# MLP second matrices in a three-layer transformer kernel: two of four row blocks as block products of seven instead of eight

## The chip, the cores and the metric

The kernel runs on one core of a Trainium2 chip. A core has a matrix engine (TensorE, PE in the rows), a vector engine (VectorE, DVE), an activation engine (ScalarE, ACT), GpSimd (POOL) and a sync engine (SP) that issues transfers here. Each works through its own list of instructions in order and waits for others by semaphores. SBUF is the on-chip memory; matmuls write to banks in PSUM. The metric is the device time of one execution in microseconds (us); less is better.

## The reference

The reference runs one block of a first model (`first_block`: convolution, stick-breaking attention and cross-attention, merged by gates, then an MLP) and two layers of a second (`hybrid_layer`: forgetting attention and retention, then an MLP). Sequence length is 256 tokens, width 1024, hidden width 4096, all in float32. The change lies in the MLPs, of which there are three:

```python
        h2 = rms_norm(x, g_mlp[l])
        x = x + jnp.square(jax.nn.relu(h2 @ w_up[l])) @ w_down[l]
...
    hid = jnp.square(jax.nn.relu(jnp.einsum('bsd,df->bsf', x, w_ff1)))
    ff = jnp.einsum('bsf,fd->bsd', hid, w_ff2)
    return layernorm(DEEPNORM_ALPHA * x + ff, ln2_g, ln2_b)
```

The second matrix of an MLP, `w_down` or `w_ff2`, has 4096 rows and 1024 columns. Four row blocks of 1024 rows are meant by the title.

## The kernel before

**Weights.** All weight matrices are packed into one stream of chunks, in the order in which they are used (`build_plan`). An up chunk of the later kind has 1024 rows and 256 columns, a down chunk 512 rows and 512 columns; both are 128 partitions x 2048 values and come in two halves of 128x1024 (512 KB). `Stream.load` (L190) has SP load halves into `RB` = 5 raw buffers. `Stream.piece` (L200) splits a half into two parts that are rounded to the matrix engine's format: ACT writes the high part, `whi` (L213), DVE the rest, `wlo` (L214). They go to one of `NB` = 5 pairs of weight buffers; during an MLP `lend` adds a sixth.

**Matmuls.** `mm3` (L320 to L322) makes each product of three matmuls: high by high, high by low, low by high. A unit (`unit_b`, four steps of 128 rows) is 12 matmuls of 512 columns, with 128 tokens as the fixed side and the weights moving. `stream_a` multiplies an up chunk with the weights as the fixed side and 256 tokens moving: 48 matmuls of 256 columns.

**An MLP** (`mlp`, L789). Four chunks of 512 columns of the first matrix come first, held together while the first 128 tokens and then the second 128 pass (`ws`). Their hidden values are transposed by PE in `tok_side`, a generator that advances one step at each `tick`. Then for each group g of 512 hidden values, 2 to 7: two up chunks (ACT takes relu and square, L800 and L801, then ACT and DVE split the values into `hid`, L312 and L306), then the two down chunks of group g-2, each for both halves of the tokens. The last four down chunks are held together. Four PSUM banks (`pd`) gather all eight groups; `half` adds a finished bank to the residual `x` at the end, in the later MLPs with a factor and a layer norm (`ln_half`, L916).

**Order.** Within an engine instructions stand as the code writes them (`manual_schedule`). Units of matmuls are the beat: each `tick` lets the open generators take a step and lets `pump` write out the split of one weight half, or two if fewer than three chunks are ready ahead. `room` says whether a weight buffer is free by then.

## Time and profile before

| | |
|---|---|
| median of 3 runs (lowest, highest) | 1223.91 us (1223.78, 1224.0) |
| the profiled execution's own time | 1223.95 us |
| its span, first to last instruction | 1222.1 us |
| PE busy | 1208.5 us, 99% |
| DVE busy | 734.8 us, 60% |
| ACT busy | 631.6 us, 52% |
| mean granted clock of PE, as a share of full speed | 0.997 |

A busy time is the sum of an engine's instruction times; on PE neighbouring matmuls overlap, so the interval between two starts, and not the length of a row, is what a matmul takes. The chain that ended last is followed back from the last instruction, at each step to what released it. A wait is named by the engine that waited and the instruction that ended the wait. The first MLP lies between about 419 and 598 us of the span.

### The profile page before, as it was taken

Reading aid. Unit: us, or ns where it says so; the run is one execution under the profiler, and the core shown is the slowest. Engines: PE = TensorE matmul, PEld = TensorE weight load, DVE = VectorE, ACT = ScalarE, POOL = GpSimd, SP = SyncE. Lnnn points to the kernel's source line nnn. Section 1 sums busy time; section 2 is a strip of 40 time slices with the busy share of each in tenths; the row PEclk is TensorE's granted clock in tenths of the full one; section 3 lists DMA queues with packets and bytes.
Section 4 is the critical chain, followed back from the end, with each engine's and each line's share of the span. In section 5 each row is a group of like instructions: output and inputs, shape, how many; then the busy total and the mean of one; then the engine's idle time right before and its main releaser. Section 6 shows DMA issues by size and latency. Waiting matters only on the chain.

```text
span 1222.1 us, 18186 instructions
## 1 busy us (share of the span) xinstructions
PE 1208.5 (99%) x7365; PEld 1059.1 (87%) x7365; DVE 734.8 (60%) x941; ACT 631.6 (52%) x887; POOL 26.2 (2%) x45
## 2 busy tenths in 40 slices
PE   8999999999999999999999999999999999999997
PEld 5999987887888888998898889899889888989985
DVE  6488775656666655355476685535567668553452
ACT  6556555545454565455255556545535555653540
POOL 1000000000000000000000100000000010000000
PEclk9999999999999999999999999999999999999999
DMA  8644446665455565556444366555545436655530
GB/s 327 224 148 144 140 156 211 233 195 162 138 172 189 184 243 208 172 172 214 156 166 139 124 214 226 197 188 173 207 130 187 146 118 216 225 193 203 167 126 35
DMA packets 60468, 218.99 MB, mean 179 GB/s; under 512 B 6848, under 2 KB 6992, under 8 KB 60384
## 3 DMA queue, kind: packets, MB, share of 16 engines
q1 hardware_dynamic: 58320, 211.12, 51.6%
q0 software_dynamic: 1776, 6.38, 1.8%
q8 instruction: 58, 0.95, 0.3%
q10 hardware_dynamic: 288, 0.33, 0.1%
q14 instruction: 26, 0.21, 0.0%
HBM read 216.75 MB, written 1.05 MB: 178 GB/s over the span
## 4 chain that ended last, share of the span: by engine, by line
PE 95%; DVE 1%; ACT 1%; DMA 1%; issue 0%; DVEq 0%; POOLq 0%; SPq 0%; ACTq 0%
PE acc L320 17%; PE acc L322 17%; PE acc L321 17%; PE bank L320 13%; PE bank L322 13%; PE bank L321 13%; PE acc L402 2%; PE acc L333 2%; PE aux L329 1%; DMA raw<-in_wpack_dram 1%; PE aux L1082 0%; DMA gmix<-in_g_mix_dram 0%; DVE wlo L214 0%; PE aux L515 0%; PE aux L322 0%
## 5 line engine op out<-in xcount | busy, mean ns | idle before, releaser
L214 DVE TENSOR_TENSOR wlo<-raw,whi 128x1024 fp32r<-128x1024 f32 x392 | 465.0, 1221 | 116.6 <-ACT whi L213 114.5
L213 ACT CAST whi<-raw 128x1024 fp32r<-128x1024 f32 x392 | 394.6, 1048 | 108.7 <-PE bank L322 58.0
L320 PE MATMUL acc<-xTh,whi 128*128 128x256 f32 x1088 | 310.6, 285 | 0.0
L321 PE MATMUL acc<-xTl,whi 128*128 128x256 f32 x1088 | 307.7, 283 | 0.0
L322 PE MATMUL acc<-xTh,wlo 128*128 128x256 f32 x1088 | 307.5, 283 | 0.0
L320 PEld LDWEIGHTS acc<-xTh,whi 128*128 128x128 f32 x1088 | 207.9, 191 | 2.7 <-issue 1.0
L321 PEld LDWEIGHTS acc<-xTl,whi 128*128 128x128 f32 x1088 | 207.9, 191 | 1.0
L322 PEld LDWEIGHTS acc<-xTh,wlo 128*128 128x128 f32 x1088 | 208.0, 191 | 0.0
L320 PE MATMUL bank<-whi,hid 128*128 128x512 f32 x384 | 151.4, 394 | 0.0
L322 PE MATMUL bank<-whi,hid 128*128 128x512 f32 x384 | 151.3, 394 | 0.0
L321 PE MATMUL bank<-wlo,hid 128*128 128x512 f32 x384 | 151.2, 394 | 0.0
L306 DVE TENSOR_TENSOR hid<-r,hid 128x512 fp32r<-128x512 f32 x36 | 24.9, 692 | 166.2 <-ACT hid L312 166.2
L800 ACT ACTIVATE r<-acc 128x512 f32<-128x512 f32 x36 | 21.5, 598 | 147.1 <-PE acc L322 147.1
L320 PE MATMUL acc<-whi,xTh 128*128 128x512 f32 x224 | 90.6, 404 | 0.7 <-ACT xTh L312 0.7
L321 PE MATMUL acc<-wlo,xTh 128*128 128x512 f32 x224 | 88.2, 394 | 1.1 <-DVE wlo L214 1.1
L322 PE MATMUL acc<-whi,xTl 128*128 128x512 f32 x224 | 88.3, 394 | 0.0
L322 PEld LDWEIGHTS bank<-whi,hid 128*128 128x128 f32 x384 | 72.2, 188 | 16.9
L320 PEld LDWEIGHTS bank<-whi,hid 128*128 128x128 f32 x384 | 72.3, 188 | 15.9
L321 PEld LDWEIGHTS bank<-wlo,hid 128*128 128x128 f32 x384 | 72.2, 188 | 16.0
L320 PE MATMUL bank<-whi,xTh 128*128 128x512 f32 (+2 forms) x192 | 68.7, 358 | 0.0
L321 PE MATMUL bank<-wlo,xTh 128*128 128x512 f32 (+2 forms) x192 | 68.1, 354 | 0.0
L322 PE MATMUL bank<-whi,xTl 128*128 128x512 f32 (+2 forms) x192 | 68.0, 354 | 0.0
(263 smaller groups left out, 1457.6 us busy)
## 6 DMA issues: line engine op xcount, KB each, us to landing
raw<-in_wpack_dram SPq DMA_DIRECT2D x388, 512.0 KB, 4.4
raw<-in_wpack_dram SPq DMA_DIRECT2D x4, 528.0 KB, 4.3
gb<-in_ln_g_dram POOLq DMA_DIRECT2D x4, 512.0 KB, 3.9
bb<-in_ln_b_dram POOLq DMA_DIRECT2D x4, 512.0 KB, 6.1
x<-in_x_dram SPq DMA_DIRECT2D x3, 512.0 KB, 7.0
mem<-in_mem_dram SPq DMA_DIRECT2D x2, 512.0 KB, 6.5
out_dram<-x SPq DMA_DIRECT2D x4, 256.0 KB, 2.2
cst<-in_c_dram POOLq DMA_DIRECT2D x1, 898.0 KB, 7.0
```

Source lines behind the costliest of these rows:

```text
L213: nc.scalar.copy(hi, raw)
L214: nc.vector.tensor_tensor(lo, raw, hi.bitcast(F32), op=ALU.subtract)
L306: nc.vector.tensor_tensor(o, x, y, op=op)
L320: nc.tensor.matmul(o, lhsT=lh, rhs=rh, start=first, stop=False, skip_group_check=True)
L321: nc.tensor.matmul(o, lhsT=lh, rhs=rl, start=False, stop=False, skip_group_check=True)
L322: nc.tensor.matmul(o, lhsT=ll, rhs=rh, start=False, stop=last, skip_group_check=True)
L329: nc.tensor.matmul(o[:, h, :], lhsT=q[a][hs[h]], rhs=k[b][hs[h]], start=i == 0, stop=i == 2, skip_group_check=True)
L333: nc.tensor.matmul(o, lhsT=l, rhs=r, start=first, stop=last, skip_group_check=True)
L402: nc.tensor.transpose(o[:, k * 128:(k + 1) * 128], src[:, k * 128:(k + 1) * 128], ident)
L800: nc.scalar.activation(dst, src, AF.Relu)
```

## The change

In each MLP the row blocks 0 and 2 of the second matrix (1024 rows) are seen as four quarters of 512x512, and the hidden values that meet them as four quarters of 128 tokens by 512. A plain product of two such 2x2 grids takes eight products of quarters; seven suffice if some of them are taken between sums and differences of quarters. `PRODUCTS` lists the seven, in order, with the weight quarter that each uses and the one that is first added to it in place.

- `w7` plans the quarters of a block as four loads and seven chunks; `Stream.add` has DVE add two raw halves (f32) ahead of the split.
- `Stream.load` issues a load when the raw buffer `RB` loads back has had its last use, so a quarter's halves stay until the last product that reads them. `RB` is 8 in place of 5. `NB` is 4 in place of 5, and no buffer is lent.
- `seven_side` makes the seven operands from the hidden values (kept whole in `hf`): DVE takes the differences, ACT and DVE split each into high and low. For block 0 it advances during the up chunks that follow, for block 2 during the down chunks of block 1.
- `seven` runs the products: 12 matmuls each, three PSUM banks; products 1, 6, 7 and 4 accumulate into one bank, 5 and 3 into a second, 2 into a third. After each product `gather` has DVE add or subtract the bank as it then stands to or from a quarter of the residual `x`.
- Row blocks 1 and 3 keep eight products; their operands are split by halves of the tokens, and block 1 too is gathered into `x` on its own, block 3 by `half`.
- The order of an MLP is now: four chunks held together, four up chunks, block 0 in seven, four up chunks, block 1, four up chunks, block 2 in seven, block 3.

```diff
-NB = 5
-RB = 5
+NB = 4
+RB = 8
...
+PRODUCTS = ((1, 0, None), (5, 0, 1), (6, 0, 2), (3, 2, None), (7, 1, 2), (2, 3, None), (4, 3, 0))
...
+    def w7(key, w, l, k0, c0, c1):
+        quarters = [(w, l, 128 * (k0 + 4 * i), 4, (c0, c1)[j], 512) for i, j in ((0, 0), (0, 1), (1, 1), (1, 0))]
+        for name, q, s in PRODUCTS:
+            plan.append(((*key, name), quarters if q == 0 and s is None else None, q, s))
...
-        for g in range(2, 8):
-            for c in (2 * g, 2 * g + 1):
+        for pair in range(1, 4):
+            for c in range(4 * pair, 4 * pair + 4):
                 wa((tag, "up", c), wu, l, 256 * c)
+            if pair % 2:
+                w7((tag, "dn", pair - 1), wd, l, 8 * (pair - 1), 0, 512)
             for n in range(2):
-                wb((tag, "dn", g - 2, n), wd, l, 512 * n, 4 * (g - 2))
-        for n in range(2):
-            for g in (6, 7):
-                wb((tag, "dn", g, n), wd, l, 512 * n, 4 * g)
+                for g in (2, 3) if pair == 2 else (6, 7) if pair == 3 else ():
+                    wb((tag, "dn", g, n), wd, l, 512 * n, 4 * g)
...
+        self.loads, self.plan = build_loads()
+        self.last = [0] * len(self.loads)
+        for c, (_, _, _, q, s) in enumerate(self.plan):
+            self.last[q] = c
+            if s is not None:
+                self.last[s] = c
+        self.dma_i = self.split_i = self.added = self.used = self.freed = self.off = 0
...
     def room(self):
         c, h = divmod(self.split_i, 2)
-        return c < len(self.plan) and (h == 1 or self.slot(c) > 0)
+        return c < len(self.plan) and (h == 1 or c < NB + self.freed)
...
     def load(self, upto=RB):
-        while self.dma_i < min(2 * len(self.plan), self.split_i + upto):
-            _, k, n = self.plan[self.dma_i // 2]
+
+        while self.dma_i < 2 * len(self.loads):
+            i, h = divmod(self.dma_i, 2)
+            j, g = divmod(self.dma_i - upto, 2)
+            if j >= 0 and 2 * self.last[j] + g >= self.split_i:
+                return
+            _, _, _, k, _, n = self.loads[i]
...
+    def add(self):
+
+        if self.added == self.split_i and self.added < 2 * len(self.plan):
+            c, h = divmod(self.added, 2)
+            _, _, _, q, s = self.plan[c]
+            if s is not None:
+                a, b = self.raws[2 * q + h], self.raws[2 * s + h]
+                self.nc.vector.tensor_tensor(a, a, b, op=ALU.add)
+            self.added += 1
+
...
         hi, lo = (t[:, h * m:(h + 1) * m] for t in self.tiles[c])
-        raw = self.raws.pop(self.split_i)
+        self.add()
+        raw = self.raws[2 * q + h]
         nc.scalar.copy(hi, raw)
+        self.split_i += 1
+        self.add()
         nc.vector.tensor_tensor(lo, raw, hi.bitcast(F32), op=ALU.subtract)
-        self.split_i += 1
         self.load()
...
-                split(hid[g][0][:, :, ts], hid[g][1][:, :, ts], p.rearrange("p (k t) -> p k t", k=4))
+                nc.scalar.copy(hf[0][:, 4 * g:4 * g + 4, ts], p.rearrange("p (k t) -> p k t", k=4))
+            if t:
+                sides.append(seven_side(0))
+
+        def seven_side(pair):
+
...
+            d, e = (r[:, 512 * i:512 * i + 512].rearrange("p (k t) -> p k t", k=4) for i in range(2))
+
+            def put(name, src):
+                o = new_op(7)
+                split(o[0], o[1], src)
+                ops[pair, name] = o
+
+            put(1, q[0, 0])
+            tt(d, q[1, 1], q[1, 0], ALU.subtract)
+            yield
+            put(5, d)
+            stt(e, d, -1.0, q[0, 0], ALU.mult, ALU.subtract)
+            yield
+            put(6, e)
+            stt(d, e, -1.0, q[0, 1], ALU.mult, ALU.subtract)
+            yield
+            put(3, d)
+            tt(e, q[0, 0], q[1, 0], ALU.subtract)
+            yield
+            put(7, e)
+            yield
+            put(2, q[0, 1])
+            yield
+            put(4, q[1, 1])
+
...
+        def gather(i, j, bank, op):
+
+            x = xtok[:, i, 512 * j:512 * j + 512]
+            stt(x, x, alpha if (i, j) not in first else 1.0, bank, ALU.mult, op)
+            first.add((i, j))
+
+        def seven(pair):
+            bk = {}
+            for name, _, _ in PRODUCTS:
+                while (pair, name) not in ops:
+                    tick(0)
+                x = ops[pair, name]
+                c = "A" if name in (1, 6, 7, 4) else "B" if name == 2 else "C"
+                fresh = c not in bk
+                if fresh:
+                    bk[c] = bank()
+                w = W.get((tag, "dn", pair, name))
+                for k in range(4):
+                    mm3(bk[c], x[0][:, k, :], x[1][:, k, :], w[0][:, k, :], w[1][:, k, :], fresh and k == 0, k == 3)
+                    if k == 1:
+                        tick()
+                W.free()
+                for i, j, op in {1: ((0, 0, ALU.add),), 5: ((1, 1, ALU.subtract),), 6: ((0, 1, ALU.subtract),),
+                                 3: ((0, 1, ALU.subtract),), 7: ((1, 1, ALU.subtract),), 2: ((0, 0, ALU.add),),
+                                 4: ((1, 0, ALU.add),)}[name]:
+                    gather(i, j, bk[c], op)
+                tick()
...
+        def down(bank, n, g, t, w):
+            o = ops[g // 2, t, g % 2]
+            for k in range(4):
+                mm3(bank, o[0][:, k, :], o[1][:, k, :], w[0][:, k, :], w[1][:, k, :], g % 2 == 0 and k == 0,
+                    g % 2 == 1 and k == 3)
...
+        for pair in range(1, 4):
+            for c in range(4 * pair, 4 * pair + 4):
+                p = stream_a((tag, "up", c), xT)
+                cc = c % 4
+                if pair == 2:
...
+                    relu2(hf[2][:, 2 * cc:2 * cc + 2, :], p)
+                    if cc == 3:
+                        sides.append(seven_side(2))
+                else:
...
+                    relu2(rv, p)
+                    for t in range(2):
+                        o = ops[pair, t, cc // 2]
+                        ks = slice(2 * (cc % 2), 2 * (cc % 2) + 2)
+                        split(o[0][:, ks, :], o[1][:, ks, :], rv[:, :, 128 * t:128 * t + 128])
                 tick()
-            if pd is None:
-                pd = [[bank(), bank()] for _ in range(2)]
-            for n in range(2):
-                w = W.get((tag, "dn", g - 2, n))
-                for t in range(2):
-                    down(g - 2, n, t, w)
-                    if t == 1:
-                        W.free()
-                    tick()
+            if pair % 2:
+                seven(pair - 1)
+            if pair == 2:
+                for n in range(2):
+                    p = [bank(), bank()]
+                    for g in (2, 3):
+                        w = W.get((tag, "dn", g, n))
+                        for t in range(2):
+                            down(p[t], n, g, t, w)
+                            if t:
+                                W.free()
+                            if g == 3:
+                                gather(t, n, p[t], ALU.add)
+                            tick()
         ws = [(W.get((tag, "dn", g, n)), g, n) for n in range(2) for g in (6, 7)]
         for t in range(2):
+            p = [bank(), bank()]
             for w, g, n in ws:
-                down(g, n, t, w)
+                down(p[n], n, g, t, w)
                 if t == 1:
...
```

PE's list is 72 matmuls shorter, the sum over six blocks of 96 less 84. On DVE two places matter. In the following rows `wlo` is the split of a weight half, `raw<-raw` the sum of two halves, `hid` and `op` splits of hidden values, `r<-` a difference of operands, `x<-x,bank` a gather, and 128x1024, 128x512 and 128x256 the sizes.

The first place is the first MLP. Before, DVE had there, from the first up chunk's hidden values on, splits of hidden values and of weight halves:

```order
L306 TENSOR_TENSOR hid_4083<-r,hid_4082 128x512
L214 TENSOR_TENSOR wlo<-raw,whi 128x1024 x6
L306 TENSOR_TENSOR hid_4301<-r,hid_4300 128x512
L214 TENSOR_TENSOR wlo<-raw,whi 128x1024 x2
L306 TENSOR_TENSOR hid_4301<-r,hid_4300 128x512
L214 TENSOR_TENSOR wlo<-raw,whi 128x1024 x6
```

Now, from the hidden values of the last up chunk ahead of the first seven-product block (two operations of 256) up to the second gather, it has:

```order
L339 TENSOR_TENSOR op_4275<-r,op_4275 128x256
L339 TENSOR_TENSOR op_4276<-r,op_4276 128x256
L339 TENSOR_TENSOR op_4355<-r,op_4355 128x512
L248 TENSOR_TENSOR wlo<-raw,whi 128x1024
L339 TENSOR_TENSOR op_4369<-hf,op_4369 128x512
L232 TENSOR_TENSOR raw<-raw 128x1024
L248 TENSOR_TENSOR wlo<-raw,whi 128x1024
L342 SCALAR_TENSOR_TENSOR x_3502<-x_3502,bank 128x512
L339 TENSOR_TENSOR op_4382<-hf,op_4382 128x512
L232 TENSOR_TENSOR raw<-raw 128x1024
L248 TENSOR_TENSOR wlo<-raw,whi 128x1024 x2
L342 SCALAR_TENSOR_TENSOR x_3502<-x_3502,bank 128x512
```

The first gather, which reads the bank that products 1 and 6 accumulate into, now stands behind four operand splits, two weight splits and a sum; the second behind one operand split, two weight splits and a sum more.

The second place is the seven-product block of the third row block, in the same MLP. Before, the same stretch of DVE's list read:

```order
L214 TENSOR_TENSOR wlo<-raw,whi 128x1024 x2
L306 TENSOR_TENSOR hid_4895<-r,hid_4894 128x512
L214 TENSOR_TENSOR wlo<-raw,whi 128x1024 x6
L306 TENSOR_TENSOR hid_5093<-r,hid_5092 128x512
L214 TENSOR_TENSOR wlo<-raw,whi 128x1024 x2
L306 TENSOR_TENSOR hid_5093<-r,hid_5092 128x512
```

Now, from the last up chunk's hidden values up to the last split ahead of the third gather:

```order
L339 TENSOR_TENSOR op_5135<-r,op_5135 128x256
L339 TENSOR_TENSOR op_5136<-r,op_5136 128x256
L248 TENSOR_TENSOR wlo<-raw,whi 128x1024
L232 TENSOR_TENSOR raw<-raw 128x1024
L248 TENSOR_TENSOR wlo<-raw,whi 128x1024
L342 SCALAR_TENSOR_TENSOR x_3502<-x_3502,bank 128x512
L232 TENSOR_TENSOR raw<-raw 128x1024
L248 TENSOR_TENSOR wlo<-raw,whi 128x1024 x2
L342 SCALAR_TENSOR_TENSOR x_3502<-x_3502,bank 128x512
L248 TENSOR_TENSOR wlo<-raw,whi 128x1024
L232 TENSOR_TENSOR raw<-raw 128x1024
L248 TENSOR_TENSOR wlo<-raw,whi 128x1024
```

Each gather stands behind two splits and a sum, and there are no operand splits between them.

## Rows read from the trace of the kernel before

**Rows 1.** The page: span, and engines with busy us, share and instructions.

```profile
span 1222.1 us, 18186 instructions
...
PE 1208.5 (99%) x7365; PEld 1059.1 (87%) x7365; DVE 734.8 (60%) x941; ACT 631.6 (52%) x887; POOL 26.2 (2%) x45
```

**Rows 2.** The page: chain that ended last, share of the span by engine.

```profile
PE 95%; DVE 1%; ACT 1%; DMA 1%; issue 0%; DVEq 0%; POOLq 0%; SPq 0%; ACTq 0%
```

**Rows 3.** PE's waits: us in total, times, longest; first and last of seven.

```profile
PE acc L402 <- DVE ht L309: 1.3, 1, 1.3
...
PE aux L320 <- ACT Tq L312: 0.3, 1, 0.3
```

**Rows 4.** Stretches of the first MLP: busy us by engine, granted clock, DMA share, GB/s.

```profile
core 0: us, PE busy (x) PEld busy (x) DVE busy (x) ACT busy (x) POOL busy (x), PEclk, DMA share, GB/s
...
465.00:487.00 22.00, 22.00 (x143) 19.95 (x142) 10.42 (x10) 11.40 (x14) 0.00 (x0) 1.00 0.50 177
...
510.00:533.00 23.00, 23.00 (x148) 20.86 (x147) 9.50 (x9) 9.40 (x12) 0.00 (x0) 1.00 0.60 203
```

**Rows 5.** Timeline of PE, 499 to 523 us: start, length, instruction.

```profile
499.75 0.39 PE L320 MATMUL bank<-whi,hid 128*128 128x512 f32 x1
...
510.81 0.28 PE L320 MATMUL acc<-xTh,whi 128*128 128x256 f32 x1
...
522.31 0.39 PE L320 MATMUL bank<-whi,hid 128*128 128x512 f32 x1
```

**Rows 6.** Timeline of DVE, 456 to 606 us; a row of xN spans N instructions.

```profile
457.56 5.76 DVE L214 TENSOR_TENSOR wlo<-raw,whi 128x1024 fp32r<-128x1024 f32 x5 [0.26 <-ACT whi L213]
...
602.02 0.69 DVE L306 TENSOR_TENSOR x<-bank,x 128x512 f32<-128x512 f32 x1
602.63 1.22 DVE L214 TENSOR_TENSOR wlo<-raw,whi 128x1024 fp32r<-128x1024 f32 x1
...
605.01 0.41 DVE L306 TENSOR_TENSOR ta<-bank,cst 128x256 f32<-128x256 f32 x1
605.34 0.42 DVE L306 TENSOR_TENSOR on<-bank,cst 128x256 f32<-128x256 f32 x1
```

**Rows 7.** Groups of DVE by line and shape: busy us, mean ns, idle before.

```profile
L916 DVE SCALAR_TENSOR_TENSOR x<-x,bank 128x512 f32<-128x512 f32 x16 | 11.0, 684 | 30.2 <-PE bank L322 30.2
```

**Rows 8.** Timeline of ACT behind the up chunk that ends at 516.56 us.

```profile
516.75 0.60 ACT L800 ACTIVATE r<-acc 128x512 f32<-128x512 f32 x1 [7.44 <-PE acc L322]
...
518.04 0.62 ACT L312 CAST hid<-r 128x512 fp32r<-128x512 f32 x1
```

**Rows 9.** Timeline of DVE behind the same chunk.

```profile
518.70 0.69 DVE L306 TENSOR_TENSOR hid<-r,hid 128x512 fp32r<-128x512 f32 x1 [7.57 <-ACT hid L312]
```

**Rows 10.** Timeline of ACT, 462 us: a cast that waited for its raw half.

```profile
462.46 1.05 ACT L213 CAST whi<-raw 128x1024 fp32r<-128x1024 f32 x1 [1.13 <-DMA raw<-in_wpack_dram]
```

**Rows 11.** Timeline of DVE, 423 us, first chunks of the first MLP.

```profile
423.67 5.76 DVE L214 TENSOR_TENSOR wlo<-raw,whi 128x1024 fp32r<-128x1024 f32 x5
```

**Rows 12.** Timeline of PE there: first matmul of the fourth chunk.

```profile
427.49 0.48 PE L320 MATMUL bank<-whi,xTh 128*128 128x512 f32 x1
```

**Rows 13.** Stretches at the start, columns as in rows 4.

```profile
8.00:12.00 4.00, 3.40 (x12) 2.04 (x13) 3.29 (x6) 3.68 (x5) 0.00 (x0) 0.74 1.02 416
12.00:16.00 4.00, 3.04 (x11) 2.09 (x9) 3.33 (x4) 3.37 (x5) 2.30 (x4) 0.83 1.03 411
```

**Rows 14.** Timeline of PE at the start.

```profile
8.08 1.32 PE L402 MATMUL acc<-ident,ht 128*128 128x128 f32 x8 [1.30 <-DVE ht L309]
9.91 0.80 PE L320 MATMUL acc<-whi,xTh 128*128 128x512 f32 x1 [0.51 <-ACT xTh L312]
...
12.30 0.63 PE L321 MATMUL acc<-wlo,xTh 128*128 128x512 f32 x1
12.73 0.63 PE L322 MATMUL acc<-whi,xTl 128*128 128x512 f32 x1
```

**Rows 15.** The page: DMA issues, count, KB each, median us to landing.

```profile
x<-in_x_dram SPq DMA_DIRECT2D x3, 512.0 KB, 7.0
```

More of the change, by code (lines that the diff above doesn't have):

```diff
@@ L148, in build_plan, with build_loads @@
     return plan
+def build_loads():
+    loads, chunks = [], []
+    for p in build_plan():
+        if len(p) == 7:
+            chunks.append((p[0], p[4], p[6], len(loads), None))
+            loads.append(p[1:])
+            continue
+        key, quarters, q, s = p
+        if quarters is not None:
+            base = len(loads)
+            loads.extend(quarters)
+        chunks.append((key, 4, 512, base + q, None if s is None else base + s))
+    return loads, chunks
 def pack_weights(inputs):
-    plan = build_plan()
-    flat = np.empty(sum(128 * k * n for _, _, _, _, k, _, n in plan), np.float32)
+    loads = build_loads()[0]
+    flat = np.empty(sum(128 * k * n for _, _, _, k, _, n in loads), np.float32)
     o = 0
-    for _, w, l, r0, k, c0, n in plan:
+    for w, l, r0, k, c0, n in loads:
         for h in range(2):
@@ L786, in block_kernel, with mlp @@
     yst.close()
-    def mlp(tag, xT, half, on_start):
+    def mlp(tag, xT, half, on_start, xtok, alpha):
         st = ExitStack()
@@ L792, in mlp, with new_op @@
         hp = pool(st, "mlp" + str(tag))
-        W.lend(pool(st, "wts" + str(tag)), (tag, "dn", 7, 1))
-        hid = {}
-        def new_hid(g):
-            hid[g] = tuple(hp.tile([128, 4, S], F32R, tag=f"hid{i}", name=f"hid{i}", bufs=3) for i in range(2))
+        ops, hf = {}, {}
+        def new_op(n):
+            t = hp.tile([128, 2, 4, 128], F32R, tag=f"op{n}", name=f"op{n}", bufs=n)
+            return t[:, 0], t[:, 1]
         def relu2(dst, src):
@@ new lines, in mlp @@
+        first = set()
+        def gather(i, j, bank, op):
[23 more added lines that the diff above has]
+                tick()
@@ L915, in ln_half @@
             cell[t] = sm.tile([128, 2], F32, tag="lsum", name="lsum")
[L916 removed]
+        nc.vector.scalar_tensor_tensor(out=xtok[:, t, ns], in0=xtok[:, t, ns], scalar=alpha, in1=bank, op0=ALU.mult,
                                        op1=ALU.add, accum_out=cell[t][:, n:n + 1])
```

62 lines of the change are left out of this document (21 added, 41 removed).

## The prediction

> **What bounds the kernel now.** I read the profile in this order: engines, chain, TensorE's waits, then stretches of the first MLP. TensorE (PE) is busy 1208.5 us of a span of 1222.1, VectorE (DVE) 734.8, ScalarE (ACT) 631.6 [rows 1]. 95% of the chain that ended last is PE [rows 2], and PE's waits for another engine are seven rows, the first of 1.3 us and the last of 0.3, 5.9 us in all [rows 3]. So PE sets the time, and a matmul taken away is worth its issue interval while the others keep up. In the first MLP they do: DVE is busy 10.42 of 22 and 9.50 of 23 us in two stretches with PE full [rows 4]. That slack is an average; the question is where in a stage the added work falls.
>
> **Prices.** In the second matrix 48 matmuls of 512 columns start from 499.75 up to 510.81, 0.230 us each; two up chunks of 48 matmuls take from 510.81 to 522.31, 5.75 us each [rows 5]. On DVE I use the interval between starts, not the duration: five splits of 128x1024 end 5.76 us after the first starts, one lasts 1.22, so (5.76-1.22)/4 = 1.14; 512 wide 602.63-602.02 = 0.61; 256 wide 605.34-605.01 = 0.33 [rows 6].
>
> **Part 1, matmuls removed.** One row block took 8 units of 12 matmuls, 96 x 0.230 = 22.1 us; now 7 x 12, a product of 12 costing 2.76 and the block 19.3. Two blocks in three MLPs: 72 matmuls, 16.6 us. That is the gain if nothing else waits.
>
> **Part 2, DVE work added, per MLP.** Splits of weight halves: 14 per block in place of 8, so 12 more. Sums: four products of each block have one, on two halves, 16 more. No row shows a sum in f32; the nearest is the split, a subtraction of the same shape on two operands, and I take its 1.14 us; from above its full 1.22, from below half of it, 0.57. Gathers: 18 of 0.61 (nearest row: the accumulation into x, 684 ns long [rows 7]). Operands: 14 splits and 8 differences of 512 and 16 splits of 256 replace 16 splits of 512. Together 13.7+18.2+11.0+13.4+5.3-9.8 = 51.8, or 155 us in three MLPs: DVE would be busy some 71% of the span. On average that fits, so the stage decides.
>
> **Part 3, the first seven-product block of an MLP.** Let 0 be the time at which PE ends the last of the four up chunks ahead of it. A chunk that ends at 510.81+5.75 = 516.56 is followed by ACT's relu at 516.75, its square, its cast at 518.04, and DVE's split of the hidden values at 518.70 [rows 8, 9]: 2.1 us; the cast is now half as wide, and I take 1.9. DVE runs in its written order, and from the second chunk's end (-11.5+1.9 = -9.6) it has, with everything it needs at hand:
> - ahead of the third chunk's hidden values: two operations of 256, four of 512, four of 1024, 0.67+2.44+4.56 = 7.7
> - ahead of the fourth's: two of 256, four of 512, three of 1024, 0.67+2.44+3.42 = 6.5
> - then two of 256, two of 512, three of 1024 and the first gather to its end, 0.67+1.22+3.42+0.69 = 6.0.
>
> That is 20.2 us, so the first gather ends at 10.6. PE waits for it: the third product accumulates into the bank that the gather of the first reads. PE has done two products by 5.5, and waits 5.1. From there DVE has one gather behind two or three operations of 1024, about 4 us against PE's 2.76: the next gathers end at 15.2, 19.2, 23.1 and, behind two splits of the next chunk, 26.1. Products three to seven start at 10.7, 15.3, 19.3, 22.1 (into a fresh bank) and 26.2; the last ends at 28.9. **28.9 against 22.1: 6.8 us lost.**
>
> The raw halves add nothing to this: the next chunk's loads take the slots whose last reader comes first (the third quarter's, free at about 9 and 12), and a load needs 3.7 us (a split from 457.56 ends at 458.78; the half that follows in its slot is cast at 462.46 [rows 6, 10]). It is wanted at 23, so there are 7 us of cover.
>
> **Part 4, the second block.** Its operands are made earlier, beside the down chunks of the second row block, so only sums, splits and gathers are in its queue. DVE starts on the last up chunk's values at 1.9, waits for ACT's cast of the next weight half until 3.2, then split, sum, split, gather: 7.3. PE waits 1.8 there, then 1.3, 1.3 and 1.4; the last product ends at 25.1. **3.0 lost.** Beside those down chunks (22 us) DVE has 8 splits, 15 operations of 512 and so 18 us, paced by PE; I cost that at nothing, and at up to 1 us a block if it slips.
>
> **Part 5, the rest.** Four weight buffers for six in the MLPs and five elsewhere, eight raw halves for five. Outside the MLPs DVE's order hardly moves, since the pump looks three chunks ahead. I cost it at nothing; the cover is PE's work on chunks already split, and it is thin where four chunks are held at once: in the first MLP five splits run from 423.67 to 429.4 [rows 11] while PE starts on the fourth chunk at 427.49 [rows 12]. If it goes, 1 to 2 us in each of some five places.
>
> **Sum.** 3 x (6.8+3.0) = 29.4 us lost, on the profiled execution's own 1223.95 (span 1222.1 plus 1.85 around it; the median is 1223.91): **1253**. With the full 1.22, 0.69 and 0.42 us for each operation the two chains grow by 3.3 and 1.1: 1266. With sums at 0.57 they lose 4.0 and 2.3: 1234. I stay with the intervals, since the nearest rows are back to back like these.
>
> The Trainium skill, "VectorE: DVE Perf Modes", section "The DRAIN you can't avoid", says that the next Vector operation does not start until the pipe has emptied, and exempts only operations that are not held; by it the full duration is the price and the sum 1266. Here starts lie 0.08 us closer than the duration [rows 6], so the trace goes with the exemption.
>
> **Rivals.** *The look-ahead suffices (faster).* DVE idles for over half of two stretches [rows 4]; were it far enough ahead that each gather is free when its product ends, the 16.6 us come whole: 1207. It decides at one point: the 20.2 us of DVE between the second up chunk and the first gather must fit into 9.6+5.5 = 15.1, and the second block's 7.3 into 5.5. Against it: four weight buffers hold a product's splits back until PE has used up a chunk, and sums stand ahead of gathers in a strict order. 0.07. If gain and waits cancel, no change: 0.05.
> *The second block costs nothing, or sums are cheap.* Then the second gives 2.8 and the first costs 6.8: 1223.95+3x4.0 = 1236; with cheap sums 1234. 0.14.
> *The clock falls.* Between 8 and 16 us the granted clock was 0.74 and 0.83 [rows 13], behind PE waits of 1.3 and 0.5 us, and matmuls of 512 columns came 0.43 us apart (12.30 to 12.73) in place of 0.23 [rows 14]: 1.2 GHz for 2.4. A product would take 5.2 us. One or two at that rate are hidden, since DVE sets the pace (the third would end at 15.9, the fourth start then in place of 15.3). All five products behind the first wait at that rate would end the blocks at 36.7 and 33.3, 48 us more in all, 1301; I take a third of that, 1269. 0.13.
> The Trainium skill, "TensorE: Matmul & The Clock Gate", section "HAM oscillation", says that idle gaps on TensorE put its clock back to half; by it the long wait at the third product could do so, which is this rival. The trace of before has no such gap after the start.
> *Weights arrive late.* One block's quarters hold all eight raw halves, and loads of the same size took 7.0 us from issue to landing [rows 15]; 3 us behind each block is 18: 1271. 0.03.
> *The change doesn't do what it says.* PE's order is 72 matmuls shorter, so it does.
>
> **How the numbers follow.** Forecast 1253 with 0.58 (1244 to 1266); smaller loss 0.14 (1230 to 1244); clock 0.13; late weights 0.03; no change 0.05; faster 0.07. A measurement of this kernel tells some 0.2% from none, 2.4 us. Slower 0.58+0.14+0.13+0.03 = 0.88, same 0.05, faster 0.07. The range leaves out the faster and unchanged cases and the outer part of the clock's: 1236 to 1273.
>
> **What would show it.** Right: in the changed profile DVE is the first among PE's waits, some 10 us at each first block and 6 at each second; the longest wait, about 5 us, stands ahead of a first block's third product and ends with the gather; DVE has no idle time from some 10 us ahead of the block to its fifth gather; outside the MLPs nothing moves. Wrong: waits on DMA or ACT there, a granted clock below 1 in those stretches, sums at half the split's price, or PE without waits and the time near 1207.

## The result and the profile after

| | before | after |
|---|---|---|
| median (lowest, highest) | 1223.85 us (1223.62, 1224.0) | 1255.62 us (1255.44, 1255.72) |
| ratio, 95% interval | | 1.026 (1.0242 to 1.0277) |
| profiled execution: own time, span | 1223.95, 1222.1 us | 1255.72, 1253.9 us |
| PE, DVE, ACT busy | 1208.5, 734.8, 631.6 us | 1204.3, 887.8, 687.0 us |
| mean granted clock | 0.997 | 0.989 |

The change makes the kernel 31.8 us slower. The page of the kernel after gives each engine's busy time with its share and instructions, and further down the chain that ended last, by engine. They answer to [rows 1, 2].

```profile
PE 1204.3 (96%) x7293; PEld 1049.2 (84%) x7293; DVE 887.8 (71%) x1145; ACT 687.0 (55%) x977; POOL 26.2 (2%) x45
...
PE 82%; DVE 11%; ACT 3%; issue 3%; DMA 1%; DVEq 0%; POOLq 0%; SPq 0%; ACTq 0%
```

The 72 matmuls are gone (7365 to 7293), and DVE has the 71% that the prediction gave it. But DVE now holds 11% of the chain where it held 1%: PE stands and waits for it somewhere. PE's waits (us in total, times, longest) say for what:

```profile
PE bank L353 <- DVE x L342: 28.4, 14, 5.1
PE bank L353 <- ACT whi L245: 7.7, 7, 1.1
```

Both rows are new against [rows 3]. The first is a matmul that accumulates into a bank which a gather (DVE, line 342, into `x`) still has to read. The second names ACT's casts of the weights, but that is only how the profile puts down a wait for several things: by the starts and ends in the timelines all 21 waits of the two rows end 0.15 us behind the end of a gather. They are all waits for gathers. The timeline of PE in the first block of the first MLP (start, length, instruction; in brackets the idle time ahead and what ended it) shows where:

```profile
471.59 0.40 PE L355 MATMUL bank<-whi,op 128*128 128x512 f32 x1
477.04 0.76 PE L353 MATMUL bank<-whi,op 128*128 128x512 f32 x1 [5.05 <-DVE x L342]
477.60 0.63 PE L354 MATMUL bank<-wlo,op 128*128 128x512 f32 x1
478.03 0.63 PE L355 MATMUL bank<-whi,op 128*128 128x512 f32 x1
...
485.84 0.47 PE L353 MATMUL bank<-whi,op 128*128 128x512 f32 x1 [1.02 <-DVE x L342]
...
492.79 0.47 PE L353 MATMUL bank<-whi,op 128*128 128x512 f32 x1 [1.11 <-DVE x L342]
...
495.65 0.28 PE L353 MATMUL acc<-xTh,whi 128*128 128x256 f32 x1
```

The block's first matmul starts at 466.25, and the third product, first to use a bank again, starts at 477.04 behind a wait of 5.05. DVE's timeline beside it shows the gather for which it waits, and what stands ahead of the next one:

```profile
473.94 1.22 DVE L232 TENSOR_TENSOR raw<-raw 128x1024 f32<-128x1024 f32 x1
475.08 1.22 DVE L248 TENSOR_TENSOR wlo<-raw,whi 128x1024 fp32r<-128x1024 f32 x1
476.21 0.68 DVE L342 SCALAR_TENSOR_TENSOR x<-x,bank 128x512 f32<-128x512 f32 x1
476.81 0.69 DVE L339 TENSOR_TENSOR op<-hf,op 128x512 fp32r<-128x512 f32 x1
477.41 1.22 DVE L232 TENSOR_TENSOR raw<-raw 128x1024 f32<-128x1024 f32 x1
478.55 2.42 DVE L248 TENSOR_TENSOR wlo<-raw,whi 128x1024 fp32r<-128x1024 f32 x2
480.89 0.68 DVE L342 SCALAR_TENSOR_TENSOR x<-x,bank 128x512 f32<-128x512 f32 x1
```

Row follows row without idle time: a sum (`raw<-raw`), splits (`wlo`), an operand, and between them the gathers, 4.68 us from the first to the second. Product one ended 2.8 us behind the block's start; its gather came 7 us later, for no reason but its place in DVE's queue. From PE's first start to its last and one more matmul, the first block takes 29.4 us (783.36 to 812.78 and 1100.58 to 1129.97 in the other MLPs, the same), and the second 25.45. Before, the eight products of row block 0 stood in two pieces. Here are the first start of each and the first start behind it, in the first MLP of the kernel before:

```profile
454.46 0.39 PE L320 MATMUL bank<-whi,hid 128*128 128x512 f32 x1
...
465.61 0.28 PE L320 MATMUL acc<-xTh,whi 128*128 128x256 f32 x1
...
477.05 0.40 PE L320 MATMUL bank<-whi,hid 128*128 128x512 f32 x1
...
488.25 0.28 PE L320 MATMUL acc<-xTh,whi 128*128 128x256 f32 x1
```

That is 11.15+11.20 = 22.35 us, and row block 2 took 22.3 in the same way. The two blocks lose 3 x (7.05+3.15) = 30.6 of the 31.8 us; the other 1.2 lie outside them.

### The profile page after: what moved, and what is told of

Same layout as the page of the kernel before. It is cut to its first block, busy times and chain, and to the rows that moved or that the text cites. A ratio compares the mean times of both kernels' runs of the same rounds, so it can differ in the third digit from the quotient of the medians.

```text
span 1253.9 us, 18383 instructions
## 1 busy us (share of the span) xinstructions
PE 1204.3 (96%) x7293; PEld 1049.2 (84%) x7293; DVE 887.8 (71%) x1145; ACT 687.0 (55%) x977; POOL 26.2 (2%) x45
## 4 chain that ended last, share of the span: by engine, by line
PE 82%; DVE 11%; ACT 3%; issue 3%; DMA 1%; DVEq 0%; POOLq 0%; SPq 0%; ACTq 0%
PE acc L353 16%; PE acc L355 15%; PE acc L354 15%; PE bank L353 10%; PE bank L354 10%; PE bank L355 9%; DVE wlo L248 5%; DVE raw L232 2%; PE acc L435 2%; PE acc L366 2%; DVE x L342 1%; DVE op L339 1%; ACT whi L245 1%; PE aux L362 1%; DMA raw<-in_wpack_dram 1%
## 5 line engine op out<-in xcount | busy, mean ns | idle before, releaser
L248 DVE TENSOR_TENSOR wlo<-raw,whi 128x1024 fp32r<-128x1024 f32 x428 | 512.2, 1220 | 127.0 <-ACT whi L245 125.8
L245 ACT CAST whi<-raw 128x1024 fp32r<-128x1024 f32 x428 | 433.5, 1049 | 160.8 <-DVE raw L232 53.4
L353 PE MATMUL bank<-whi,op 128*128 128x512 f32 x360 | 146.7, 408 | 36.0 <-DVE x L342 28.4
L354 PE MATMUL bank<-wlo,op 128*128 128x512 f32 x360 | 144.4, 401 | 0.0
L355 PE MATMUL bank<-whi,op 128*128 128x512 f32 x360 | 144.2, 401 | 0.0
L353 PEld LDWEIGHTS bank<-whi,op 128*128 128x128 f32 x360 | 69.4, 193 | 59.6 <-ACT whi L245 35.4
L355 PEld LDWEIGHTS bank<-whi,op 128*128 128x128 f32 x360 | 69.3, 192 | 16.5
L354 PEld LDWEIGHTS bank<-wlo,op 128*128 128x128 f32 x360 | 69.5, 193 | 14.9
L232 DVE TENSOR_TENSOR raw<-raw 128x1024 f32<-128x1024 f32 x48 | 58.5, 1220 | 0.5
L339 DVE TENSOR_TENSOR op<-r,op 128x256 fp32r<-128x256 f32 (+1 forms) x72 | 34.1, 508 | 33.6 <-ACT op L345 33.6
```

The costliest lines, as they stand in the source:

```text
L232: self.nc.vector.tensor_tensor(a, a, b, op=ALU.add)
L245: nc.scalar.copy(hi, raw)
L248: nc.vector.tensor_tensor(lo, raw, hi.bitcast(F32), op=ALU.subtract)
L339: nc.vector.tensor_tensor(o, x, y, op=op)
L353: nc.tensor.matmul(o, lhsT=lh, rhs=rh, start=first, stop=False, skip_group_check=True)
L354: nc.tensor.matmul(o, lhsT=lh, rhs=rl, start=False, stop=False, skip_group_check=True)
```

## The experiments

A ratio stands with its 95% interval; all runs are against the kernel before, which took 1223.6 to 1223.9 in each set. This table gathers what the timelines show of the two blocks (row blocks 0 and 2) in the first MLP, measured as above; e1 to e12 are the runs below. Without any wait a block of seven is 84 x 0.232 = 19.5 us.

| run | first block | second block | time, us |
|---|---|---|---|
| before (eight products) | 22.35 | 22.3 | 1223.9 |
| after | 29.4 | 25.45 | 1255.6 |
| e2: only the second block in seven | eight | 25.4 | 1234.2 |
| e3: no sums | 22.4 | 20.6 | 1220.2 |
| e4: a bank for each product | 24.4 | 20.5 | 1227.3 |
| e5: sums on GpSimd | 36.0 | 29.6 | 1288.3 |
| e6: PE kept busy in the long wait | 29.4 | 25.5 | 1255.7 |
| e7: sums by adding DMA | 33.3 | 31.9 | 1290.0 |
| e8: operands earlier | 28.6 | 25.5 | 1253.4 |
| e9: sums doubled | 39.2 | 34.3 | 1307.3 |
| e10: gathers ahead of weights | 27.0 | 22.5 | 1238.4 |
| e11: e10, e8 and splits put off | 23.9 | 22.5 | 1235.2 |
| e12: splits let in by a table | 21.5 | 21.0 | 1236.5 |

**Is it the buffers?** The kernel before with the changed buffer counts and nothing else.

```diff
-NB = 5
-RB = 5
+NB = 4
+RB = 8
```

(and the call that lends a sixth buffer is gone.)

> The kernel before with four weight buffers and eight raw halves, nothing lent; plain products everywhere. DVE's queue in the seven-product blocks is the cause (theory): the buffers cost nothing, 1224 us, within 1222 to 1227. Rival, that fewer weight buffers hold PE up: a good part of the 32 us comes here, 1235 or more.

Measured 1224.84, ratio 1.001 (1.0001 to 1.0019): 1.0 us, between 0.1 and 2.3. The buffers by themselves are not the cause.

**Does each block cost what it was said to?** The first block goes back to eight products; the second stays in seven.

```diff
-            if pair % 2:
+            if pair == 3:
...
```

> The changed kernel with row block 0 back to eight products and only row block 2 in seven. Theory: the first block's operand splits stand in the same DVE queue and make it the dear one; what is left is three second blocks of 25.4 us in place of 22.1, 1224 + 3 x 3.3 and some 1 to 2 us around them, 1235. Rival, that a seven-product block costs the same wherever it stands: half of the 32 us, 1240. Rival, that the second blocks cost nothing by themselves: 1216.

Measured 1234.18, ratio 1.0085 (1.007 to 1.010). The second blocks cost 10.4 us, which leaves 21.4 for the first ones. The waits of the second block are those of the kernel after: the longest is 1.7.

**Is it the sums?** The kernel without them; four of its products use the bare quarter.

```diff
-            if s is not None:
-                a, b = self.raws[2 * q + h], self.raws[2 * s + h]
-                self.nc.vector.tensor_tensor(a, a, b, op=ALU.add)
```

> The changed kernel without the sums of raw halves (four of the seven products use the bare quarter). Theory: with 16 x 1.14 us less per MLP ahead of the gathers, the first block ends at about 21.2 us and the second at about 20.3 in place of 29.4 and 25.4: 1217, within 1212 to 1222. Rival, that PE waits for buffers, banks or the clock and not for DVE's time: 1245 or more.

Measured 1220.23, ratio 0.9971 (0.9959 to 0.9982). Less 54.7 us of DVE (48 x 1.14) makes 35.4 us less time. PE's first wait shrinks to this:

```profile
PE bank L350 <- DVE x L339: 8.3, 9, 1.7
```

So even with sums for nothing the change would have won 3.6 of its 16.6 us: the first block, with its operands, its six more splits and its gathers, takes 22.4, as long as with eight products.

**Is it the shared bank?** Every product gets a bank of its own, so that no matmul waits for a gather. The sums over products are left out by this.

```diff
-                fresh = c not in bk
-                if fresh:
-                    bk[c] = bank()
+                fresh = True
+                bk[c] = bank()
```

> The changed kernel with a fresh PSUM bank for every product, so that no product waits for the gather of an earlier one (the sums over products are left out). DVE's work and order are the same. Theory: PE then waits only for the splits in the same queue; the first block ends at about 25.3 in place of 29.4, the second at 21.5 in place of 25.4, in all 1233 to 1234. Rival, that the splits themselves are what PE waits for: 1255. Rival, that the shared bank is all of the loss: 1208.

Measured 1227.33, ratio 1.003 (1.0019 to 1.0041), better than I expected. DVE's queue is as it was: the gather that started at 476.21 starts here at 476.15, but nobody waits for it. 28.3 of the 31.8 us are paid only where a gather stands between two products in one bank. What is left is another wait, for the weights themselves:

```profile
PE bank L354 <- DVE wlo L248: 12.2, 11, 1.8
```

**Can GpSimd take the sums?**

```diff
-                self.nc.vector.tensor_tensor(a, a, b, op=ALU.add)
+                self.nc.gpsimd.tensor_tensor(a, a, b, op=ALU.add)
```

> The changed kernel with the sums on GpSimd in place of DVE, in the same places. Theory: DVE has 18 us less per MLP; if a sum takes GpSimd up to some 2.5 us and does not slow DVE, the blocks end at about 21.2 and 20.3 us: 1217. If GpSimd is slower or takes DVE's memory port, sums come late and the time lies between 1225 and 1255. Rival, that DVE's time is not the cause: 1250 or more.

Measured 1288.29, ratio 1.0525 (1.0508 to 1.0543), in the rival's range, but not for the rival's reason, and far above what I gave to a slow GpSimd. The groups of instructions by line and shape (busy us, mean ns of one, idle before) show two costs:

```profile
L232 POOL TENSOR_TENSOR raw<-raw 128x1024 f32<-128x1024 f32 x48 | 132.8, 2788 | 360.0 <-DVE wlo L248 360.0
L339 DVE TENSOR_TENSOR op<-r,op 128x256 fp32r<-128x256 f32 x48 | 48.4, 1048 | 30.2 <-ACT op L345 30.2
L342 DVE SCALAR_TENSOR_TENSOR x<-x,bank 128x512 f32<-128x512 f32 x54 | 36.8, 682 | 5.3 <-PE bank L355 5.3
L342 DVE SCALAR_TENSOR_TENSOR r<-r,hf 128x512 f32<-128x512 f32 x12 | 21.3, 1772 | 0.0
```

A sum takes 2.79 us on GpSimd (1.22 on DVE), and the splits behind it wait for it. And DVE's own operations get longer: the split of 256 goes from 420 ns to 1048, the difference `r<-r,hf` from 683 to 1772. The gather, of the same instruction and shape as that difference, stays at 682 (680 in the kernel after). The two differ in where their second operand lies: `hf` in SBUF, `bank` in PSUM. DVE is busy 905.3 us here and 887.8 in the kernel after: taking the sums off DVE gave it more to do, not less.

**Can the DMA take them?** Each sum is an adding DMA between raw halves, issued as soon as the earlier reader of the same quarter has been split.

```diff
...
-                self.nc.vector.tensor_tensor(a, a, b, op=ALU.add)
+                self.nc.gpsimd.dma_start(out=a, in_=b, accum_op=ALU.add)
...
```

> The sums of weight quarters are made by adding DMAs (out = out + in, between raw halves in SBUF, issued from GpSimd's queue) in place of DVE instructions, each issued as soon as the product ahead of it that reads the same quarter has been split; all else is as in the kernel after. Theory (DVE's work in the block, with the sums in it, sets the time): DVE's queue is as in the run without sums, which took 1220, so 1218 to 1230 if the adding DMA lands in about the 4 to 5 us that a raw half takes from DRAM, since products five and six then follow a split by one such landing each. Rival (the sums must be somewhere, and where they move they are waited for): landings of 10 us or more put ScalarE's and DVE's splits of the second and third product late by some 5 us each in each of six blocks, and the time is 1250 or more, with PE waits that name the casts of the weights and no longer the gathers.

Measured 1289.97, ratio 1.0538 (1.052 to 1.0556): the rival's number without its condition, landings of 10 us or more. The page (DMA issues: count, KB each, median us to landing), and the timelines of GpSimd and of DVE in the first block:

```profile
raw<-raw POOLq DMA_DIRECT2D x48, 512.0 KB, 5.4
```

```profile
480.51 0.85 POOL L237 DMA_DIRECT2D raw<-raw  x1 [15.19 <-DVE wlo L252]
```

```profile
487.02 1.23 DVE L252 TENSOR_TENSOR wlo<-raw,whi 128x1024 fp32r<-128x1024 f32 x1 [5.07 <-ACT whi L250]
...
493.50 0.68 DVE L347 SCALAR_TENSOR_TENSOR x<-x,bank 128x512 f32<-128x512 f32 x1
```

A landing takes 5.4 us, nearly what I had allowed. But the block's last sum adds into the quarter that the product named 2 (the sixth) has just split, so it is issued at 480.51 and no sooner, and DVE's queue, which runs in order, stands 5.07 us at the split of that sum with the gathers behind it. PE stands too, 5.61 us, until 494.32, 0.15 us behind the gather that starts at 493.50. (PE's rows name casts for 33.5 us of waits, the rival's sign, but these waits too end 0.15 us behind a gather.) The sums left DVE's busy time and not its queue.

**Does the clock cost anything?** In the long wait of the first block PE's clock falls. Stretches of the first MLP in the kernel after (us, busy of PE, PEld, DVE, ACT, POOL, granted clock, DMA share, GB/s):

```profile
474.00:478.00 4.00, 0.96 (x2) 0.83 (x3) 4.00 (x6) 1.05 (x1) 0.00 (x0) 0.56 0.42 118
478.00:482.00 4.00, 4.00 (x12) 3.13 (x11) 4.00 (x5) 2.94 (x3) 0.00 (x0) 0.58 0.58 188
482.00:486.00 4.00, 2.98 (x14) 2.13 (x13) 3.97 (x5) 1.05 (x1) 0.00 (x0) 1.00 0.81 265
```

In the third product matmuls start 0.43 us apart (477.60 to 478.03 above), the lower level of 1.2 GHz. The next run fills most of the wait with matmuls into a bank that nobody reads.

```diff
+                if name == 6 and pair == 0:
+                    spare = acc()
+                    for i in range(18):
+                        nc.tensor.matmul(spare, lhsT=y[0][:, i % 4, :], rhs=y[0], start=True, stop=True,
+                                         skip_group_check=True)
+                y = x
```

> The changed kernel with 18 matmuls into an unused bank between the second and third product of each first block, so that PE is at work during the wait of 5 us (their result is not used). Theory: the clock stays up, the third product takes 2.8 us in place of 4.8, and the fourth starts when its gather allows, 0.3 us sooner: 1254.7, three times 0.3 below the changed kernel. Rival, that the clock's fall is part of the loss: 3 x 2 us sooner, 1250.

Measured 1255.67, ratio 1.026 (1.0245 to 1.0275). Its PE timeline:

```profile
472.18 4.29 PE L900 MATMUL acc<-op 128*128 128x512 f32 x18
477.40 0.48 PE L353 MATMUL bank<-whi,op 128*128 128x512 f32 x1 [0.93 <-DVE x L342]
...
482.08 0.47 PE L353 MATMUL bank<-whi,op 128*128 128x512 f32 x1 [1.64 <-ACT whi L245]
```

The third product starts where it did (10.79 us into the block in both), runs at full clock (granted 1.00 from 478 to 482 us) and ends 2.0 us sooner, and the fourth then waits 1.64 us and starts only 0.15 us sooner. The row names a cast, but the wait ends 0.15 us behind the second gather, which the fourth product needs. The clock's fall in this block costs nothing.

**How much of DVE's added time is paid?** Each sum is followed by a second instruction of its size.

```diff
                 self.nc.vector.tensor_tensor(a, a, b, op=ALU.add)
+                self.nc.vector.tensor_tensor(a, a, a, op=ALU.max)
```

> Each of the 48 sums is followed by one more DVE instruction of its size that leaves the sum as it is (the larger of it and itself), so DVE has twice the cost of the sums and nothing else changes. Without the sums the time was 1220.2, with them 1255.6: 35.4 us for 48 x 1.14 = 54.7 us of DVE, 0.65 us of the end for each us of the sums. Theory (the sums take idle time of DVE ahead of the blocks first and are then paid whole): the second dose is paid at more than the first, 0.65 to 1.0: 1291 to 1310. Rival (it is less the sums' own time than the one step in which a product's weights wait for its sum, so that work in DVE's queue is mostly hidden): 0.4 or less, 1277 or below.

Measured 1307.31, ratio 1.0677 (1.0659 to 1.0695). No sums 1220.2, sums once 1255.6, twice 1307.3: of the first 54.7 us of DVE 65% are paid, of the second 95%. By the pages (span less busy time, in which instructions that overlap count once, and are not summed) DVE idles 386.1 us without the sums, 366.1 with them and 361.2 with twice their cost: the first dose still finds idle time of DVE, the second hardly any. TensorE's clock falls more often in this run, too (mean granted clock 0.972 for 0.989); how much of the second dose is the clock's is not shown.

**Is it the block's late start on DVE?**

```diff
-            yield
-            yield
+            if t == 0:
+                yield
+                yield
...
-            r = hp.tile([128, D], F32, tag="r", name="r", bufs=2)
+            r = hp.tile([128, 512], F32, tag="rs", name="rs", bufs=1)
...
```

> The operands of the first block of seven begin about 6 us earlier: the second half of hidden block 0 is transposed two steps earlier, and the differences have a 2 KB tile of their own, so the seven operands are made beside the first up chunks of the stage and not its last ones. The work of every engine stays the same. Theory (DVE's queue sets the first block: it is packed from 9.6 us ahead of the block to its end, while between 442 and 456.7 it idles 5 to 6 us): the idle time is filled, the first gather and all behind it come 3 to 6 us earlier, the wait ahead of the third product shrinks from 5.05 us to 2 or less, and the three first blocks end 3 to 5.5 us earlier each: 1239 to 1247. Rival (inside the block a product needs more of DVE than PE's 2.8 us, and the block's end is set by that pace from its own first gather, or by the weights that four buffers let in): the third product's wait goes and comes back at the fourth and fifth, and the time stays at 1253 to 1256.

Measured 1253.36, ratio 1.0239 (1.0224 to 1.0254). By its time that is the rival's, but the trace says that the edit hardly did what it was for: DVE is packed from 450.81 where it was from 456.66, but from 442 us to there it had idled for 6.1 us and still idles for 4.7, so only 1.4 us of work were moved forward, and the first gather starts at 475.94 for 476.21. It leaves open what a truly earlier start would bring.

**Is it the order in DVE's queue?** Inside the block only the next product's weights are split ahead.

```diff
+AHEAD = 2
...
-            if self.room():
+            if self.room() and (ahead is None or self.split_i < 2 * self.used + ahead):
...
-                        tick()
+                        tick(1, AHEAD)
...
```

> Only the order of DVE's (and ScalarE's) queue inside a block of seven changes: there the stream splits no more than one product's weights beyond the running one (two halves, in place of the six that the four buffers let in), so that a gather stands behind one or two splits and sums and no longer behind those of three products; what is put off comes after the block. The work of every engine is the same. Theory (a gather is late because of the weights queued ahead of it, of which some belong to chunks behind the block): laying the measured starts of DVE's rows (1.14 for a sum or split, 0.61 and 0.33 for operands, 0.60 for a gather) end to end in the new order gives 24.9 us for the first block (29.9 by the same count in the old order, 29.4 measured) and 22.9 for the second (25.6, and 25.4 measured), 7.7 less per MLP: about 1232, 1228 to 1238. Rival (lookahead of weights is what keeps PE fed, and with two halves each product waits for its own split): the waits name the casts and splits of the weights, and the time is 1250 or more.

Measured 1238.43, ratio 1.012 (1.0105 to 1.0135). No engine has less to do, and 17.2 of the 31.8 us are gone. The two waits of the kernel after have given way to these:

```profile
PE bank L355 <- DVE wlo L249: 12.0, 14, 1.2
PE bank L354 <- DVE x L343: 8.3, 3, 2.8
```

So more than half of the loss is a matter of order: splits for products and chunks further on stood ahead of gathers that PE needed at once. It fell 6 us short of my count. In the first MLP the wait of 2.78 us ahead of the third product was again followed by the lower clock (rows 0.43 us apart from 475.39 on), which here put off the end; in the two other MLPs the same wait was not.

**What else stands ahead of the gathers?** To e10 and e8 this run adds that the splits of the hidden values of the last two up chunks go behind the block.

```diff
+                    if cc > 1:
+                        lates.append(late)
...
             if pair % 2:
                 seven(pair - 1)
+                while lates:
+                    lates.pop(0)()
```

> As the run with the gathers ahead of the weights, and besides the operands of the first block begin earlier, as in the run of that name, and the splits of hidden block 1's last two up chunks, which nothing needs in the block, go behind it. Theory (all that counts is what stands in DVE's queue ahead of the gathers that PE needs): by the same count of DVE's rows the first block takes 22.3 us, its first gather ends 6.2 us behind the block's start (10.6 measured in the kernel after), and the second block 22.9 as in the other run: three MLPs at 45.2 in place of 54.8, 28.8 us less: about 1227, 1224 to 1234, so at best what the kernel before took. If DVE's total work and not its order holds the blocks, it gives nothing over the other run.

Measured 1235.18, ratio 1.0094 (1.0077 to 1.0111). The first block falls to 23.9, and the remaining wait for a gather is one of 1.1 to 1.2 us in each MLP; 15.1 us of PE's waits are now for splits of weights. But it put off the same splits behind the second block too, where block 3 needs them at once: from the second block's end to block 3's the kernel after takes 22.95 us and this one 24.5, three times 1.6 given back.

**How far does order carry?** Splits are let in one half at a time by a table, and two gathers for which no product waits go behind the block.

```diff
+CAPS = (7, 7, 8, 9, 9, 11, 11, 12, 12, 14, 14, 15, 15, 15)
...
-                    gather(i, j, bk[c], op)
+                    held.append((name not in (3, 2), i, j, bk[c], op))
+                    if held[-1][0]:
+                        gather(*held.pop()[1:])
...
```

> The same seven products, in the run before this one's order with four edits to DVE's queue in the blocks: the splits of the weights are let in one half at a time by a table, so that each gather stands where PE has just ended its product; the gathers of the products named 3 and 2, for which no later product waits, go behind the block; the first operand of hidden block 0 is split one step earlier; and the late splits of hidden block 3 go back to where they were, since the products right behind the second block read them (1.3 us lost there in each MLP). Theory (order of DVE's queue): by the count of rows that gave 23.4 and 22.3 us for the last order (23.9 and 22.5 measured), the first block takes 21.5 to 22.7 and the second 20.2 to 20.7, against 22.1 each before the change: 1219, 1216 to 1226, no slower than the kernel before. Rival (DVE's load, near 71% of the span with the sums in, comes back as waits behind the blocks, where the splits that were put off now fall): 1230 or more, with PE's waits in the up chunks and in the last down block.

Measured 1236.48, ratio 1.0102 (1.0085 to 1.0119). The first block did what was counted, 21.5, and the second came close with 21.0: together 2.1 us less than two blocks of eight. The time did not follow, and the rival said why. The timeline of PE behind the first block of the second MLP:

```profile
802.15 0.58 PE L356 MATMUL acc<-xTh,wlo 128*128 128x256 f32 x1 [2.77 <-DVE wlo L249]
802.53 0.42 PE L354 MATMUL acc<-xTh,whi 128*128 128x256 f32 x1
802.75 0.41 PE L355 MATMUL acc<-xTl,whi 128*128 128x256 f32 x1
```

and the stretch behind that wait:

```profile
803.00:808.00 5.00, 5.00 (x25) 5.00 (x25) 1.37 (x2) 0.00 (x0) 0.00 (x0) 0.50 0.94 299
```

The up chunk's weights were among the splits put off; PE stands 2.77 us for them, and then runs its next matmuls 0.21 us apart in place of 0.12, since the clock is down to a half, with no DVE to hide behind. From the first block's last start to row block 1's first it is 26.3, 28.9 and 27.8 us in the three MLPs against 23.3, and behind the second block some 1.8 more: 18 of the 37 us that the blocks had won. A table with one more half ahead at the block's end was not tried. No order that was run beats the kernel before.

## Why the prediction was right

*Part 1* holds: 72 matmuls less and 84 of 0.232 us where nothing waits. Its price for a row block of eight, 22.1, is that of row block 1, from which [rows 5] are; blocks 0 and 2 took 22.35 and 22.3.

*Part 2* holds. A sum is a split's price: 48 of 1220 ns, start to start 1.14 (473.94 to 475.08).

*Part 3* holds almost to the row. From the block's first start at 466.25, the first gather ends at 476.89, 10.6 as forecast, and the wait is 5.05 for 5.1. Products three to seven start at 10.8, 15.6, 19.6, 22.5 and 26.5 (10.7, 15.3, 19.3, 22.1, 26.2), and the block ends at 29.4 for 28.9. Of the 0.3 at the fourth half is the clock's fall (without it, in e6, it starts at 15.5), which the rival had put at 15.9. DVE's chain is the cause in the sense of e9 and e10: more work in it is paid at 95%, and another order of the same work takes away more than half of the loss.

*Part 4* holds: a first gather at 7.3, and these waits, here in the timeline of PE:

```profile
571.43 0.48 PE L353 MATMUL bank<-whi,op 128*128 128x512 f32 x1 [1.69 <-DVE x L342]
575.50 0.47 PE L353 MATMUL bank<-whi,op 128*128 128x512 f32 x1 [1.04 <-ACT whi L245]
579.63 0.47 PE L353 MATMUL bank<-whi,op 128*128 128x512 f32 x1 [1.09 <-DVE x L342]
586.58 0.47 PE L353 MATMUL bank<-whi,op 128*128 128x512 f32 x1 [1.14 <-ACT whi L245]
```

I had 1.8, 1.3, 1.3 and 1.4, all of them for gathers. Two rows name a cast, but DVE's timeline has a gather that ends 0.15 us ahead of each of these two starts, as ahead of the others:

```profile
574.68 0.68 DVE L342 SCALAR_TENSOR_TENSOR x<-x,bank 128x512 f32<-128x512 f32 x1
...
585.75 0.68 DVE L342 SCALAR_TENSOR_TENSOR x<-x,bank 128x512 f32<-128x512 f32 x1
```

The block ends at 25.45 for 25.1.

*Part 5* was costed at nothing; by itself it is 1.0 us (e1).

*The sum* came out 2.6 us short of 1255.6. The mis-sized terms are the two blocks' ends, 0.5 and 0.35 later than forecast, 2.55 us in three MLPs. Two smaller slips nearly cancel: the price of eight products is 0.45 higher in the two blocks, 1.35 in three MLPs, and 1.2 of the 31.8 us lie outside the blocks, where I had nothing. So the loss in the blocks is 10.2 per MLP for 9.8. As for the ends, a wait costs PE some 0.25 us beyond its row (the starts around the second wait are 484.42, 485.84 and 486.15: 1.42 less the row's 1.02 and a matmul's 0.23, and then 0.31 for 0.23), and I left that out. PE's rows of waits hold 36.1 us, 12.0 per MLP, where I expected some 16: what the clock's fall hides and what a restart costs stand in no row of waits.

*The rivals.* That the look-ahead suffices falls at the point named: 20.2 us of DVE did not fit into 15.1. Cheap sums fall by their rows. The clock did fall, to a half in the third product of every first block (granted 0.50 from 794 to 798 and from 1112 to 1116 us in the other two MLPs), but in one product only and under DVE's cover, as the text on that rival allowed; e6 shows that it is free there. Late weights do not show: no DMA is among PE's waits, nor among those of ACT's casts around the six blocks. Of the signs that I had named for being wrong, a clock below 1 did appear, and by e6 it carries none of the loss; the waits on ACT (7.7 us) are so by name alone.

## What to carry to other kernels

A product saved on the engine that sets the time is worth its price only if what the saving needs on a second engine has a place in that engine's queue; lay out that queue row by row in the stage itself, since 71% of a span says nothing about 30 us of it. In a queue that runs in order, ask of each instruction who waits for it now: a look-ahead that fills every free buffer puts next stage's work ahead of this stage's. And what is put off must land where somebody has time for it, or it comes back as a wait in the next stage.

## What the runs showed of the hardware that I had not expected

Sums moved to GpSimd cost DVE more time than they took off it. With 48 sums of 2.79 us on GpSimd, DVE was busy 905.3 us, against 887.8 with the sums on DVE and 832.9 without any. Of DVE's operations with two operands in SBUF some took up to 2.6 times as long on average (683 to 1772 ns), while the gathers, with one in PSUM, kept their 682, also the 24 of them that ran beside a sum on GpSimd. The Trainium skill, "SBUF — State Buffer", section "Who interferes with whom", says that a DVE instruction with two SBUF inputs contends with a GpSimd instruction that reads SBUF, and one with at most one such input, outside the 2-port modes, does not; these rows agree. "GPSIMD Engine Reference" of the Trainium skill, section "3.1 Elementwise — side-by-side cycle accounting", gives an f32 addition of 2048 values 1.96 times DVE's time on GpSimd. The shortest of the sums here, of 1024 values, took 2.40 us, 1.97 times DVE's 1.22, which agrees; the mean of all 48 was 2.29 times (2788 to 1220 ns).

The granted clock does not answer alike to like waits. A wait of 2.78 us ahead of the third product was followed by the lower level in one of e10's three MLPs and by full clock in two. What a fall costs depends on what PE waits for next: nothing in the first block of the kernel after, and in e12, behind the block, some 2.6 us in the second MLP (28.9 against 26.3 in the first, which had the same wait and kept its clock).
